# A Mamba-2 and attention trunk: four head pairs to one TensorE visit, y written over the convolved x, and a longer planned distance for TensorE's side work

## The chip, the cores and the metric

The kernel runs on one core of one Trainium2 chip. The metric is the device time of one execution in microseconds (us). Before the change it is 1143.38 us, the median of three runs (1142.94 to 1145.92). The profile is of one execution of its own.

## What is computed

The input x is 256 rows of 2048 numbers in fp32. The first layer is a Mamba-2 layer, the second is attention; both add their result to the stream, and a norm ends the trunk.

```python
def mamba2_layer(h, w_in, ...):                 # h = rmsnorm(x), 256 x 2048
    proj = h @ w_in                             # 2048 x 10304: z, xBC (x, B, C), dt
    xbc = silu(causal_depthwise_conv(xbc, conv_w, conv_b))      # 4 taps
    dt = softplus(dt + dt_bias);  a = dt * -exp(A_log)
    y = ssd_chunked_scan(x * dt, a, B, C)       # one chunk of 256: per head,
        # y = ((C B^T) * exp(a_cum[l] - a_cum[s]), causal) @ (x * dt)
    y = y + D_skip * x                          # 64 heads of 64 channels, 8 groups
    y = grouped_rmsnorm(y * silu(z), gnorm_g)   # over each group's 512 channels
    return y @ w_out                            # 4096 x 2048
...
k, v = rope(..), ..  = split(rmsnorm(x) @ w_kv)            # 2048 x 4096
q, z = rope(..), ..  = split(rmsnorm(x) @ w_in)            # 2048 x 4096
x = x + (causal_attention(q, k, v) * silu(z)) @ w_out      # 16 heads of 128
out = rmsnorm(x)
```

With 256 rows there is one attention block, so the block selection of the reference picks nothing but that block.

## The kernel before

**Products.** All the big products run in blocks of 512 output columns. A block has two halves of 128 rows and goes through its weights in units of 256 rows by 512 columns. `load` brings a unit to the tile `raw` (four buffers), `split` makes of it `hi` (ScalarE rounds it to fp32r) and `lo` (VectorE takes the difference), and `products` issues three products of 512 columns for each 128 rows and each half: x-high by hi, x-low by hi, x-high by lo. There are 384 such units and so 4608 products, which all write tiles named `ps`. The list `ORDER` gives the order of the first layer's blocks; the second layer has four K, four V, and then the blocks "z0 q0 q1 z1 q2 q3 z2 z3" of gates and queries.

**Side work.** Everything else (convolution, decay matrices, norms, rope, attention) is written as generators. After each three products `some(2)` advances up to two of them by a step. `Paced` wraps TensorE, ScalarE and VectorE, adds up a planned time for each instruction, and so keeps three planned clocks while the program is being written out. `Side.some` advances a generator only if what it did last is planned to end `MARGIN` (750 ns) before TensorE's planned clock, and nothing at all while an engine is planned over `LAG` (1000 ns) ahead of TensorE. The order on each engine is fixed by this when the program is built; on the chip only semaphores hold it. Helper instructions all carry line 126, the line in `Paced` that calls the engine.

**The scan, group by group.** For each group g of eight heads (four pairs), `conv_gen` makes the convolved x in a slot `xs` and its transposed, dt-weighted copy `xd`; `cb_gen` makes C B^T (tile `cb`). A `pair_gen` for each pair copies two rows of a_cum over all partitions (a copy on the GpSimd queue from the small DRAM tensor `AC` to a slot `em`, 256 KB), takes the exponent and multiplies by `cb`. At every second pair it does TensorE's part for two pairs, in a PSUM bank each: eight matmuls with a 64-column stationary operand, two heads writing the two halves of the 128 partitions. I call such a stretch between products a visit. Then VectorE makes y = x*D + that, in a slot `yt`, and y*0.5*z with the gate. `norm_gen` squares, sums and normalizes y into the operand `yn`. Slots: `xs` three, `em` two, `yt` two, PSUM banks for side work (`s`) four.

**Between the layers.** `x1_gen` transposes the new stream by 128 columns (index k, 0 to 15) and writes the operand `kvop`; `r1_gen` computes the norm's factors, transposes them (`s<-ident,r`), copies them to `rB`, and writes `csr` (rope's table times the factor), then `bop`, the second layer's operand.

Of the kernel before, what the change touches and what calls it, by code (L numbers as in the profile page):

```python
# [15 lines left out]
P = 128  # L16
# [12 lines left out]
MAIN_BANKS = 4  # L29
LAG = 1000.0  # L30
MARGIN = 750.0


ORDER = "B0 d0 C0 x0 z0 x1 z1 x2 z2 x3 z3 B1 o0 C1 o1 x4 o2 z4 x5 o3 z5 x6 o10 z6 x7 o11 z7 o12 o13 p0 p1 p2 p3".split()
# [95 lines left out]
class Side:  # L130
# [8 lines left out]
    def advance(self, entry):  # L139
        gen, ready, _ = entry  # L140
        if ready is not None and not ready():
            return 0
        before = [e.ns for e in self.engines]
        at = 0.0
        try:
            entry[1] = next(gen)
            if isinstance(entry[1], float):
                at, entry[1] = entry[1], None
        except StopIteration:
            self.gens.remove(entry)  # L150
        entry[2] = max([at] + [e.ns for e, b in zip(self.engines, before) if e.ns > b])
        return 1

    def some(self, most):


        PE = self.engines[0]
        for entry in list(self.gens):
            if most <= 0 or any(e.ns > PE.ns + LAG for e in self.engines):
                return  # L160
            if entry[2] <= PE.ns - MARGIN:
                most -= self.advance(entry)

    def step(self):
# [5 lines left out]
def trunk_kernel(ctx: ExitStack, tc: tile.TileContext, x, a_norm_g, a_w_in, a_conv_w, a_conv_b,  # L170
# [31 lines left out]
    def dram(t, offset, ap):  # L202
# [6 lines left out]
    psum = ctx.enter_context(tc.tile_pool(name="psum", bufs=1, space=bass.MemoryType.PSUM))  # L209
    scratch = ExitStack()  # L210
    work = scratch.enter_context(tc.tile_pool(name="ssd", bufs=2, reuse_waits="tile"))
    S = [Slots(work, {"T": ([P, 512], 2), "u": ([P, 4, L], 1), "xs": ([P, 4, L], 3), "xd": ([P, 2, 512], 1),
                      "cb": ([P, 384], 4), "em": ([P, 2, 384], 2), "z": ([P, 1024], 1), "yt": ([P, 4, L], 2)})]
    banks = Slots(psum, {"s": ([P, 512], 8 - MAIN_BANKS)}, clock.banks)
    spare = Parts(big, "U", "y5", [P, 1024], 2)
    B = {}
# [5 lines left out]
        return next(s for s in (banks, S[0], spare) if tag in s.shape)  # L222

    def can(*tags):
        return lambda: all(of(t).free(t) > 0 for t in tags)

    def take(tag):
        return of(tag).take(tag)
# [177 lines left out]
        return a.rearrange("p j (b l) -> p j b l", l=32)  # L406


    ga = const.tile([16, P], F32, name="ga")
    SP.dma_start(ga, dram(a_norm_g, 0, [[P, 16], [1, P]]))  # L410
    xl = [big.tile([P, D], F32, name=f"xl{t}", tag=f"y{4 + t}") for t in range(2)]
    xv = x[0].rearrange("(t p) d -> p t d", p=P)
# [85 lines left out]
    warm_up()  # L498
    nt = const.tile([P, 4, 2], F32, name="r0")
    r0 = nt[:, 2, :]  # L500

    def squares(h):

# [4 lines left out]
    def first_norm():  # L508
        DVE.tensor_reduce(nt[:, 0, :], ss, axis=mybir.AxisListType.X, op=OP.add)
        root(nt, D)  # L510

    gv = const.tile([P, 112], F32, name="gv")
    cbias = const.tile([P, 48], F32, name="cbias")
# [63 lines left out]
    def dt_gen(w):  # L577
        u, m, e, s, s2 = (w[0:64, i, :] for i in range(5))
        DVE.scalar_tensor_tensor(m, u, -1.0, u, op0=OP.mult, op1=OP.min)
        yield  # L580
        ACT.activation(e, m, AF.Exp)
        yield
        DVE.tensor_scalar(m, e, 2.0, None, op0=OP.add)
        DVE.reciprocal(s2, m)
        DVE.tensor_mul(s, e, s2)
        yield
        DVE.tensor_mul(s2, s, s)
        DVE.tensor_scalar(m, s2, 1.0 / 17, None, op0=OP.mult)
# [24 lines left out]
        for t in range(2):  # L613
            PE.transpose(p[:, t, :], b[:, t * P:(t + 1) * P], ident)
        yield
        dal = const.tile([P, 2, P], F32, name="dal", tag="c2")
        ACT.activation(dal, p, AF.Copy)
        give(p)
        st["dal"] = dal
# [69 lines left out]
                side.add(cb_gen(q), lambda: ("B", q) in st and ("C", q) in st)  # L689
        return evac  # L690

    def pair_gen(g, j):

        c = 4 * g + j
        E = take("em")
        AC = st["AC"]
        R = bass.AP(tensor=AC.tensor, offset=AC.offset + 2 * c * L, ap=[[0, P], [L, 2], [1, L]])
        POOL.dma_start(E[:, :, :L], R)
        yield copied(E)
        yield lambda: "dal" in st  # L700
        dal = st["dal"]
        for h in range(2):
            a = 64 + 2 * c + h
            ACT.activation(E[:, h, 256:384], E[:, h, P:L], AF.Relu, bias=dal[:, 1, a:a + 1], scale=-1.0)
            ACT.activation(E[:, h, 0:256], E[:, h, 0:256], AF.Relu, bias=dal[:, 0, a:a + 1], scale=-1.0)
        ACT.activation(E, E, AF.Exp, scale=-1.0)
        yield lambda: ("cb", g) in st
        DVE.tensor_mul(E, E, st["cb", g][:, None, :].to_broadcast([P, 2, 384]))
        st["em", g, j], when["em", g, j] = E, clock.last
        if j % 2:  # L710
            yield lambda: ("xd", g) in st and ("em", g, j - 1) in st
            yield max(when["xd", g], when["em", g, j - 1])
            yield lambda: of("s").free("s") > 1 and (("y", g) in st or can("yt")())
            for i in (j - 1, j):
                xd, E, q = st["xd", g], st.pop(("em", g, i)), take("s")[:, :L]
                for h in range(2):
                    PE.matmul(q[h * 64:(h + 1) * 64, :], lhsT=xd[:, 0, i * P + h * 64:i * P + (h + 1) * 64],
                              rhs=E[:, h, 0:256], start=True, stop=False)
                for h in range(2):
                    PE.matmul(q[h * 64:(h + 1) * 64, P:L], lhsT=xd[:, 1, i * P + h * 64:i * P + (h + 1) * 64],  # L720
                              rhs=E[:, h, 256:384], start=False, stop=True)
                give(E)
                st["q", g, i], when["q", g, i] = q, clock.last
            if ("y", g) not in st:
                st["y", g], st["n", g] = take("yt"), 0
            yield
        else:
            yield lambda: ("q", g, j) in st
            yield when["q", g, j]
        xd, xs, q = st["xd", g], st["xs", g], st.pop(("q", g, j))  # L730
        y = st["y", g][:, j, :]
        DVE.scalar_tensor_tensor(y, xs[:, j, :], Dv[:, c:c + 1], q, op0=OP.mult, op1=OP.add)
        give(q)
        st["x", g] = st.get(("x", g), 0) + 1
        if st["x", g] == 4:
            give(xs, xd, st["cb", g])
        yield lambda: ("z", g) in st
        z = st["z", g]
        y = y.rearrange("p (b l) -> p b l", l=32)
        DVE.scalar_tensor_tensor(y, y, 0.5, by_channel(z)[:, j], op0=OP.mult, op1=OP.mult)  # L740
        st["n", g] += 1
        if st["n", g] == 4 and g not in (1, 3):
            give(z)

    def norm_gen(g):
# [37 lines left out]
    def z_gen(U, there, g):  # L783
# [5 lines left out]
        else:  # L789
            yield can("z")  # L790
            z = take("z")
        ACT.activation(z, U, AF.Tanh, scale=0.5)
        yield
        DVE.scalar_tensor_tensor(z, z, 1.0, U, op0=OP.add, op1=OP.mult)
        give(U)
# [1 line left out]

    def z_evac(g):
        def evac(ps, t):
            U, there = turn(ps, t, r0)  # L800
            if t:
                side.add(z_gen(U, there, g))
        return evac

    def x_evac(g):
        base = conv_evac(4 * g, ("xs", g), g)

        def evac(ps, t):
            base(ps, t)
            if not t:  # L810
                return
            for j in range(4):
                side.add(pair_gen(g, j), lambda: "AC" in st and can("em")())
            side.add(norm_gen(g), lambda: st.get(("n", g)) == 4)
        return evac

# [66 lines left out]
    def r1_gen():  # L883
# [16 lines left out]
        ACT.activation(rB, R, AF.Copy)  # L900
        give(R)
        yield
        csr = const.tile([P, 2, L], F32, name="csr", tag="c2")
        DVE.tensor_mul(csr, B["cs"], rB[:, None, :].to_broadcast([P, 2, L]))
        B["csr"] = csr
        bop = [big.tile([P, 4, 2 * L], F32R, name=f"bop{i}", tag=f"y{i}") for i in range(4)]
# [81 lines left out]
    def att_gen(half, there, h0):  # L988
# [57 lines left out]
                      start=False, stop=True)  # L1046
        give(E)
        yield
        if ("z", h0) not in st:
# [5 lines left out]
            yield lambda: ("z", h0) in st  # L1055
        gate = st.pop(("z", h0))
        DVE.tensor_mul(gate.heads, in_32s(o), gate.heads)
        give(o)
        yield
# [12 lines left out]
    def gate_gen(U, there, n):  # L1072
# [7 lines left out]
            DVE.scalar_tensor_tensor(U[:, c], th, 1.0, U[:, c], op0=OP.add, op1=OP.mult)  # L1080
            give(th)
        for i, half in enumerate(two(U)):
            st["z", 4 * n + 2 * i] = half

    def zb_evac(n):
        def evac(ps, t):
# [9 lines left out]
        block(w_kv, 2 * D, 512 * n, range(16), lambda k: B["kvop"][:, k, :], "x", k_evac(n), "kv")  # L1096
    for n in range(4):
        block(w_kv, 2 * D, D + 512 * n, range(16), lambda k: B["kvop"][:, k, :], "x", v_evac(n), "kv")
    for kind, n in ("z0", "q0", "q1", "z1", "q2", "q3", "z2", "z3"):
        n = int(n)  # L1100
        if kind == "q":
            block(b_w_in, 2 * D, 512 * n, range(16), b_op, "x", q_evac(n), "b")
# [145 lines left out]
```

## Time and profile before

| what | value |
|---|---|
| median of three runs | 1143.38 us |
| the profiled execution: its own time, its span | 1143.61 us, 1141.9 us |
| TensorE busy, share of the span | 99% |
| VectorE, ScalarE, GpSimd busy | 73%, 56%, 11% |
| granted TensorE clock, mean | 0.997 of full speed |
| moved from and to HBM, over the span | 226 GB/s |
| chain that ended last: `ps` products, side work of TensorE (`s`) | 90% and 6% of the span |

The span runs from the first to the last instruction; the own time of an execution has some time around it (1.7 us here). Matmuls are recorded with their latency and overlap, so what one costs is read from start to start, not from its duration. A matmul of two fp32 operands is recorded as two rows, so eight matmuls of a visit show as x16.

### The profile page before, as it was taken

What the parts mean: (1) busy time and instruction counts of PE and PEld (TensorE: products, weight loads), DVE (VectorE), ACT (ScalarE), POOL (GpSimd) and SP (SyncE); (2) the same over time, 40 slices, a digit from 0 to 9 for tenths busy, and PEclk for the clock granted to TensorE, in tenths of its full rate; (3) what the DMA queues carried; (4) which work ended last, traced back from release to release, by engine and by line L of the source; (5) the groups of instructions that cost most, each with busy time, mean ns of one, the idle gap of its engine ahead of it and who ended that gap; (6) DMA issues with size and microseconds to landing.
All of it is one profiled execution on the core that took longest, in us unless ns stands there. A gap on an engine that the chain in (4) does not pass through costs nothing.

```text
span 1141.9 us, 14900 instructions
## 1 busy us (share of the span) xinstructions
PE 1130.1 (99%) x5217; PEld 923.2 (81%) x5217; DVE 839.2 (73%) x1283; ACT 641.6 (56%) x890; POOL 124.4 (11%) x217
## 2 busy tenths in 40 slices
PE   9999999999999999999999999999999999999996
PEld 6888888888888888888878888888888888888885
DVE  5787878778799878787877558876445597887564
ACT  5666566767656666667554655434343444445353
POOL 2011112012011111101000000000000012122000
PEclk9999999999999999999999999999999999999998
DMA  8787888878778777777765467768658688888852
GB/s 263 222 242 242 249 229 278 268 243 253 210 222 240 223 237 225 237 234 231 215 232 177 162 197 218 224 200 261 220 174 244 209 248 237 263 250 261 254 185 92
DMA packets 130363, 258.91 MB, mean 227 GB/s; under 512 B 12976, under 2 KB 13824, under 8 KB 129904
## 3 DMA queue, kind: packets, MB, share of 16 engines
q1 hardware_dynamic: 119232, 226.01, 63.2%
q0 software_dynamic: 11056, 31.95, 10.9%
q8 instruction: 41, 0.67, 0.2%
q14 instruction: 34, 0.28, 0.1%
HBM read 235.83 MB, written 22.09 MB: 226 GB/s over the span
## 4 chain that ended last, share of the span: by engine, by line
PE 96%; DMA 1%; DVE 1%; ACT 0%; SPq 0%; issue 0%; ACTq 0%; DVEq 0%
PE ps L126 90%; PE s L126 6%; DMA raw<-in_a_w_in_dram 1%; PE ps_dt L126 0%; DVE xs L126 0%; DVE lo L126 0%; ACT hi L126 0%; SPq L416 0%; DVE x L126 0%; DVE T L126 0%; SPq L306 0%; ACT T L126 0%; ACT x L126 0%; DVE sfin L126 0%; ACTq L1243 0%
## 5 line engine op out<-in xcount | busy, mean ns | idle before, releaser
L126 DVE TENSOR_TENSOR lo<-raw,hi 128x1024 fp32r<-128x1024 f32 (+1 forms) x385 | 462.7, 1215 | 192.1 <-ACT hi L126 189.1
L126 ACT ACTIVATE hi<-raw 128x1024 fp32r<-128x1024 f32 (+1 forms) x385 | 397.7, 1052 | 263.3 <-PE ps L126 137.5
L126 PE MATMUL ps<-hi,hT 128*128 128x512 f32 x1280 | 401.1, 394 | 0.5 <-ACT hi L126 0.4
L126 PEld LDWEIGHTS ps<-hi,hT 128*128 128x128 f32 x1280 | 235.6, 188 | 49.2 <-issue 2.1
L126 PE MATMUL ps<-lo,hT 128*128 128x512 f32 x640 | 249.8, 390 | 0.0
L126 PE MATMUL ps<-hi,bop 128*128 128x512 f32 x512 | 161.1, 396 | 0.0
L126 PE MATMUL ps<-hi,yn 128*128 128x512 f32 x512 | 159.7, 393 | 0.0
L126 PE MATMUL ps<-hi,kvop 128*128 128x512 f32 x512 | 158.2, 390 | 0.0
L397 POOL DMA_DIRECT2D U<-turned x128 | 74.3, 587 | 748.9 <-DMA turned<-T 408.2
L126 PEld LDWEIGHTS ps<-lo,hT 128*128 128x128 f32 x640 | 120.1, 188 | 26.4 <-DVE lo L126 0.9
L126 PEld LDWEIGHTS ps<-hi,kvop 128*128 128x128 f32 x512 | 95.7, 188 | 19.7
L126 PEld LDWEIGHTS ps<-hi,bop 128*128 128x128 f32 x512 | 95.8, 188 | 19.4
L126 PEld LDWEIGHTS ps<-hi,yn 128*128 128x128 f32 x512 | 94.7, 188 | 19.4 <-issue 0.5
L126 PE MATMUL ps<-lo,yn 128*128 128x512 f32 x256 | 99.8, 390 | 0.0
L126 PE MATMUL ps<-lo,bop 128*128 128x512 f32 x256 | 99.8, 390 | 0.0
L126 PE MATMUL ps<-lo,kvop 128*128 128x512 f32 x256 | 99.7, 389 | 0.0
L126 PE MATMUL ps<-hi,oop 128*128 128x512 f32 x256 | 78.9, 390 | 0.0
L126 DVE STREAM_TRANSPOSE T<-ps 128x512 f32<-128x512 f32 x64 | 43.4, 699 | 25.6 <-ACT ps L126 15.9
L126 DVE SCALAR_TENSOR_TENSOR xs<-u,cw,xs 128x255 f32<-128x255 f32 (+2 forms) x144 | 59.7, 475 | 0.0
L126 ACT ACTIVATE em<-em,dal 128x128 f32<-128x128 f32 (+1 forms) x128 | 54.4, 449 | 5.0 <-DMA em<-AC 2.9
L126 PEld LDWEIGHTS ps<-lo,bop 128*128 128x128 f32 x256 | 48.0, 188 | 10.3
L126 PEld LDWEIGHTS ps<-lo,yn 128*128 128x128 f32 x256 | 48.0, 188 | 10.1
(165 smaller groups left out, 922.5 us busy)
## 6 DMA issues: line engine op xcount, KB each, us to landing
raw<-in_a_w_in_dram SPq DMA_DIRECT2D x159, 512.0 KB, 5.3
raw<-in_a_w_out_dram SPq DMA_DIRECT2D x64, 512.0 KB, 4.8
raw<-in_w_kv_dram SPq DMA_DIRECT2D x64, 512.0 KB, 4.8
raw<-in_b_w_in_dram SPq DMA_DIRECT2D x64, 512.0 KB, 4.7
turned<-T SPq DMA_DIRECT2D x64, 256.0 KB, 4.3
U<-turned POOLq DMA_DIRECT2D x128, 128.0 KB, 6.5
raw<-in_b_w_out_dram SPq DMA_DIRECT2D x32, 512.0 KB, 4.9
em<-AC POOLq DMA_DIRECT2D x32, 256.0 KB, 6.0
```

The source lines that it names most:

```text
L126: return call(out, *args, **kw)
L397: POOL.dma_start(U[32 * q:32 * q + 32].rearrange("p (b c) -> p b c", b=8), src)
```

## The change

- `MARGIN_PE`, 3000 ns: a step that waits for a PSUM bank (`can` with "s"), that is TensorE's side work, is advanced only if what its generator did last is planned to end 3000 ns before TensorE's planned clock. Other steps keep 750 ns. `advance` no longer forgets an earlier planned end at a step that issues nothing.
- `pair_gen` is split. `em_gen` makes the decay matrix of one pair. `y_gen` waits for all four pairs of a group, takes two PSUM banks and issues all sixteen matmuls (32 recorded rows) in one visit, two pairs to a bank. VectorE writes y over the convolved x in `xs`, and multiplies by the gate for two pairs at a time.
- Slots: `xs` four, `em` four, `yt` none. Four `em` copies can be under way at once where two could.
- The 0.5 of the gate moves to the factor `r0h` that scales z, and out of the tanh and the last product.
- `ga` and `dal` share another constant slot, and `csr` gets a place of its own. Attention's gates have the name "gate" in the table `st`, where "z" was also the first layer's. The second layer's blocks stand as "z0 q0 q1 q2 z1 q3 z2 z3".

```diff
+MARGIN_PE = 3000.0
...
-        entry[2] = max([at] + [e.ns for e, b in zip(self.engines, before) if e.ns > b])
+        entry[2] = max([entry[2], at] + [e.ns for e, b in zip(self.engines, before) if e.ns > b])
...
-            if entry[2] <= PE.ns - MARGIN:
+            if entry[2] <= PE.ns - (MARGIN_PE if getattr(entry[1], "pe", False) else MARGIN):
                 most -= self.advance(entry)
...
-    S = [Slots(work, {"T": ([P, 512], 2), "u": ([P, 4, L], 1), "xs": ([P, 4, L], 3), "xd": ([P, 2, 512], 1),
-                      "cb": ([P, 384], 4), "em": ([P, 2, 384], 2), "z": ([P, 1024], 1), "yt": ([P, 4, L], 2)})]
+    S = [Slots(work, {"T": ([P, 512], 2), "u": ([P, 4, L], 1), "xs": ([P, 4, L], 4), "xd": ([P, 2, 512], 1),
+                      "cb": ([P, 384], 4), "em": ([P, 2, 384], 4), "z": ([P, 1024], 1)})]
...
     def can(*tags):
-        return lambda: all(of(t).free(t) > 0 for t in tags)
+        def ready():
+            return all(of(t).free(t) >= tags.count(t) for t in tags)
+        ready.pe = "s" in tags
+        return ready
...
+        DVE.tensor_scalar(r0h, r0, 0.5, None, op0=OP.mult)
...
         st["em", g, j], when["em", g, j] = E, clock.last
...
-            yield lambda: of("s").free("s") > 1 and (("y", g) in st or can("yt")())
-            for i in (j - 1, j):
-                xd, E, q = st["xd", g], st.pop(("em", g, i)), take("s")[:, :L]
...
+    def y_gen(g):
+
+        yield lambda: ("xd", g) in st and st.get(("ems", g)) == 4
+        yield max(when["xd", g], *(when["em", g, j] for j in range(4)))
+        yield can("s", "s")
+        xd, y = st["xd", g], st["xs", g]
+        Q = []
+        for i in (0, 2):
+            q = take("s").rearrange("p (j l) -> p j l", j=2)
+            Q.append(q)
+            for j in (i, i + 1):
+                E = st.pop(("em", g, j))
                 for h in range(2):
+                    PE.matmul(q[h * 64:(h + 1) * 64, j - i, :], lhsT=xd[:, 0, j * P + h * 64:j * P + (h + 1) * 64],
                               rhs=E[:, h, 0:256], start=True, stop=False)
...
-        DVE.scalar_tensor_tensor(y, xs[:, j, :], Dv[:, c:c + 1], q, op0=OP.mult, op1=OP.add)
...
-        DVE.scalar_tensor_tensor(y, y, 0.5, by_channel(z)[:, j], op0=OP.mult, op1=OP.mult)
...
+                DVE.scalar_tensor_tensor(y[:, j, :], y[:, j, :], Dv[:, c:c + 1], Q[i // 2][:, j - i, :],
+                                         op0=OP.mult, op1=OP.add)
+            give(Q[i // 2])
...
+            DVE.tensor_mul(v, v, by_channel(z)[:, i:i + 2])
...
-        csr = const.tile([P, 2, L], F32, name="csr", tag="c2")
+        csr = p.tile([P, 2, L], F32, name="csr", bufs=1)
...
-    for kind, n in ("z0", "q0", "q1", "z1", "q2", "q3", "z2", "z3"):
+    for kind, n in ("z0", "q0", "q1", "q2", "z1", "q3", "z2", "z3"):
```

The change adds one line above the helpers, so line 126 of before is line 127 of the change.

The first place is TensorE's first visit for y (`s<-em,xd`, of group 0) among the products (`ps`). Before:

```order
L126 MATMUL ps<-lo,hT 128x512
L126 MATMUL s<-em,xd 64x256 x2
L126 MATMUL s<-em,xd 64x128 x2
L126 MATMUL s<-em,xd 64x256 x2
L126 MATMUL s<-em,xd 64x128 x2
L126 MATMUL ps<-hi,hT 128x512 x2
```

In the change, at the same place:

```order
L127 MATMUL ps<-lo,hT 128x512
L127 MATMUL s<-em,xd 64x256 x2
L127 MATMUL s<-em,xd 64x128 x2
L127 MATMUL s<-em,xd 64x256 x2
L127 MATMUL s<-em,xd 64x128 x2
L127 MATMUL s<-em,xd 64x256 x2
L127 MATMUL s<-em,xd 64x128 x2
L127 MATMUL s<-em,xd 64x256 x2
L127 MATMUL s<-em,xd 64x128 x2
L127 MATMUL ps<-hi,hT 128x512 x2
```

The first layer has 16 visits of the first kind before, and 8 of the second kind in the change; the matmuls in them are the same in number and shape.

The second place is TensorE in the first K block, where the norm's factors are transposed (`s<-ident,r`). Before, the last transposes of the stream (`s<-ident,x`, k = 15) stand six groups of three products ahead of it:

```order
L126 MATMUL ps<-hi,kvop 128x512 x2
L126 MATMUL ps<-lo,kvop 128x512
L126 MATMUL s<-ident,r_6034 128x128 x2
L126 MATMUL ps<-hi,kvop 128x512 x2
L126 MATMUL ps<-lo,kvop 128x512
```

In the change:

```order
L127 MATMUL s<-ident,r_6020 128x128 x2
L127 MATMUL ps<-hi,kvop 128x512 x2
L127 MATMUL ps<-lo,kvop 128x512
L127 MATMUL ps<-hi,kvop 128x512 x2
L127 MATMUL ps<-lo,kvop 128x512
L127 MATMUL s<-ident,x_1480 128x128
L127 MATMUL s<-ident,x_1481 128x128
L127 MATMUL ps<-hi,kvop 128x512 x2
L127 MATMUL ps<-lo,kvop 128x512
```

The transposes for k = 15 now come two groups behind the factors, and the first products that read k = 15 are the fourth group after them; before, fifteen groups lay between.

The third place is VectorE there, from the table `csr` on. Before:

```order
L126 TENSOR_SCALAR r1h<-r_6034 128x2
L126 TENSOR_TENSOR lo<-raw,hi 128x1024
L126 TENSOR_TENSOR csr<-cs,rB 128x512
L126 SCALAR_TENSOR_TENSOR x1T_5512<-x1T_5512,gv,rB 128x256 x2
L126 TENSOR_TENSOR lo<-raw,hi 128x1024
```

In the change:

```order
L127 SCALAR_TENSOR_TENSOR kvop<-s,gv,kvop 128x256
L127 TENSOR_TENSOR lo<-raw,hi 128x1024
L127 TENSOR_TENSOR csr<-cs,rB 128x512
L127 SCALAR_TENSOR_TENSOR x1T_5474<-x1T_5474,gv,rB 128x256 x2
L127 SCALAR_TENSOR_TENSOR kvop<-s,gv,kvop 128x256
L127 TENSOR_TENSOR bop_6107<-x1T_5474,bop_6107 128x2x256
```

The low half of k = 15 (the second `kvop` row) now stands behind `csr` and two rows that wait for `rB`; before, it stood ahead of them.

## Rows read from the trace of the kernel before

**Rows 1.** Page, part 5: costliest groups: ScalarE's hi (busy, mean ns | idle before).

```profile
L126 ACT ACTIVATE hi<-raw 128x1024 fp32r<-128x1024 f32 (+1 forms) x385 | 397.7, 1052 | 263.3 <-PE ps L126 137.5
```

**Rows 2.** TensorE's waits, whole span: us in total, times, longest.

```profile
PE s L126 <- DVE early L126: 1.2, 1, 1.2
PE s L126 <- DMA xl<-in_x_dram: 0.5, 1, 0.5
PE ps L126 <- ACT hi L126: 0.4, 1, 0.4
```

**Rows 3.** Chain of waits: start us, us, what.

```profile
689.20 228.51 PE ps L126 x1008
1132.52 0.02 issue
```

**Rows 4.** Timeline, TensorE, first visit for y: start us, us.

```profile
139.76 0.39 PE L126 MATMUL ps<-lo,hT 128*128 128x512 f32 x1
140.08 1.52 PE L126 MATMUL s<-em,xd 128*64 128x256 f32 x16
141.53 0.73 PE L126 MATMUL ps<-hi,hT 128*128 128x512 f32 x2
142.10 0.39 PE L126 MATMUL ps<-lo,hT 128*128 128x512 f32 x1
```

**Rows 5.** Timeline, TensorE, inside that visit (narrow windows, last heads and second pair).

```profile
140.67 0.49 PE L126 MATMUL s<-em,xd 128*64 128x128 f32 x4
...
140.78 0.39 PE L126 MATMUL s<-em,xd 128*64 128x256 f32 x2
...
141.32 0.28 PE L126 MATMUL s<-em,xd 128*64 128x128 f32 x2
```

**Rows 6.** Timeline, TensorE, a visit for y with cb matmuls behind it.

```profile
355.73 0.39 PE L126 MATMUL ps<-lo,hT 128*128 128x512 f32 x1
356.05 1.52 PE L126 MATMUL s<-em,xd 128*64 128x256 f32 x16
...
358.72 0.40 PE L126 MATMUL ps<-lo,hT 128*128 128x512 f32 x1
```

**Rows 7.** Timeline, TensorE, the first and the second visit for cb.

```profile
98.98 0.39 PE L126 MATMUL ps<-lo,hT 128*128 128x512 f32 x1
...
100.71 0.40 PE L126 MATMUL ps<-lo,hT 128*128 128x512 f32 x1
...
110.25 0.39 PE L126 MATMUL ps<-lo,hT 128*128 128x512 f32 x1
...
111.58 0.39 PE L126 MATMUL ps<-lo,hT 128*128 128x512 f32 x1
```

**Rows 8.** Timeline, TensorE, two visits of a norm's squares.

```profile
235.36 0.39 PE L126 MATMUL ps<-lo,hT 128*128 128x512 f32 x1
...
236.27 0.39 PE L126 MATMUL ps<-lo,hT 128*128 128x512 f32 x1
...
303.32 0.40 PE L126 MATMUL ps<-lo,hT 128*128 128x512 f32 x1
...
304.36 0.40 PE L126 MATMUL ps<-lo,hT 128*128 128x512 f32 x1
```

**Rows 9.** Timeline, TensorE, ScalarE and VectorE, from the factors' transposes on.

```profile
688.82 0.38 PE L126 MATMUL s<-ident,r 128*128 128x128 f32 x2
...
689.29 0.39 ACT L126 ACTIVATE rB<-s 128x256 f32<-128x256 f32 x1 [0.42 <-PE s L126]
...
690.31 0.68 DVE L126 TENSOR_TENSOR csr<-cs,rB 128x512 f32<-128x512 f32 x1
690.91 0.87 DVE L126 SCALAR_TENSOR_TENSOR x1T<-x1T,gv,rB 128x256 f32<-128x256 f32 x2
...
686.09 0.48 DVE L126 SCALAR_TENSOR_TENSOR kvop<-s,gv,kvop 128x256 fp32r<-128x256 f32 x1
```

**Rows 10.** Windows: us, busy of PE, PEld, DVE, ACT, POOL, clock, DMA share, GB/s.

```profile
100.00:300.00 200.00, 200.00 (x955) 162.88 (x954) 154.68 (x233) 134.09 (x182) 28.23 (x46) 1.00 0.85 251
```

More of the change, by code (lines that the diff above doesn't have):

```diff
@@ L406, in in_32s @@
         return a.rearrange("p j (b l) -> p j b l", l=32)
-    ga = const.tile([16, P], F32, name="ga")
+    ga = const.tile([16, P], F32, name="ga", tag="c1")
     SP.dma_start(ga, dram(a_norm_g, 0, [[P, 16], [1, P]]))
@@ L500, in trunk_kernel @@
     r0 = nt[:, 2, :]
+    r0h = const.tile([P, 2], F32, name="r0h")
     def squares(h):
@@ L615, in dt_gen @@
         yield
-        dal = const.tile([P, 2, P], F32, name="dal", tag="c2")
+        dal = const.tile([P, 2, P], F32, name="dal", tag="c1")
         ACT.activation(dal, p, AF.Copy)
@@ L690, in c_evac, with em_gen @@
         return evac
-    def pair_gen(g, j):
+    def em_gen(g, j):
         c = 4 * g + j
@@ L709, in pair_gen @@
         st["em", g, j], when["em", g, j] = E, clock.last
-        if j % 2:
-            yield lambda: ("xd", g) in st and ("em", g, j - 1) in st
-            yield max(when["xd", g], when["em", g, j - 1])
-            yield lambda: of("s").free("s") > 1 and (("y", g) in st or can("yt")())
-            for i in (j - 1, j):
-                xd, E, q = st["xd", g], st.pop(("em", g, i)), take("s")[:, :L]
+        st["ems", g] = st.get(("ems", g), 0) + 1
+        if st["ems", g] == 4:
+            give(st["cb", g])
@@ L718, in pair_gen @@
                               rhs=E[:, h, 0:256], start=True, stop=False)
                 for h in range(2):
-                    PE.matmul(q[h * 64:(h + 1) * 64, P:L], lhsT=xd[:, 1, i * P + h * 64:i * P + (h + 1) * 64],
+                    PE.matmul(q[h * 64:(h + 1) * 64, j - i, P:L], lhsT=xd[:, 1, j * P + h * 64:j * P + (h + 1) * 64],
                               rhs=E[:, h, 256:384], start=False, stop=True)
                 give(E)
-                st["q", g, i], when["q", g, i] = q, clock.last
@@ L724, in pair_gen @@
-            if ("y", g) not in st:
-                st["y", g], st["n", g] = take("yt"), 0
+        give(xd)
+        for i in (0, 2):
             yield
[L727 to L731, printed above, removed]
-        DVE.scalar_tensor_tensor(y, xs[:, j, :], Dv[:, c:c + 1], q, op0=OP.mult, op1=OP.add)
-        give(q)
-        st["x", g] = st.get(("x", g), 0) + 1
@@ L735, in pair_gen @@
-        if st["x", g] == 4:
-            give(xs, xd, st["cb", g])
+            for j in (i, i + 1):
+                c = 4 * g + j
+                DVE.scalar_tensor_tensor(y[:, j, :], y[:, j, :], Dv[:, c:c + 1], Q[i // 2][:, j - i, :],
+                                         op0=OP.mult, op1=OP.add)
+            give(Q[i // 2])
         yield lambda: ("z", g) in st
         z = st["z", g]
-        y = y.rearrange("p (b l) -> p b l", l=32)
-        DVE.scalar_tensor_tensor(y, y, 0.5, by_channel(z)[:, j], op0=OP.mult, op1=OP.mult)
@@ L741, in pair_gen @@
-        st["n", g] += 1
-        if st["n", g] == 4 and g not in (1, 3):
+        for i in (0, 2):
+            v = y[:, i:i + 2, :].rearrange("p j (b l) -> p j b l", l=32)
+            DVE.tensor_mul(v, v, by_channel(z)[:, i:i + 2])
+            yield
+        st["y", g] = y
+        st["n", g] = 4
+        if g not in (1, 3):
             give(z)
@@ L791, in z_gen @@
             z = take("z")
-        ACT.activation(z, U, AF.Tanh, scale=0.5)
+        ACT.activation(z, U, AF.Tanh)
         yield
@@ L799, in evac @@
         def evac(ps, t):
-            U, there = turn(ps, t, r0)
+            U, there = turn(ps, t, r0h)
             if t:
@@ L812, in evac @@
             for j in range(4):
-                side.add(pair_gen(g, j), lambda: "AC" in st and can("em")())
+                side.add(em_gen(g, j), lambda: "AC" in st and can("em")())
+            side.add(y_gen(g))
             side.add(norm_gen(g), lambda: st.get(("n", g)) == 4)
@@ L1048, in att_gen @@
         yield
-        if ("z", h0) not in st:
+        if ("gate", h0) not in st:
             yield can("q")
@@ L1054, in att_gen @@
             o = z
-            yield lambda: ("z", h0) in st
-        gate = st.pop(("z", h0))
+            yield lambda: ("gate", h0) in st
+        gate = st.pop(("gate", h0))
         DVE.tensor_mul(gate.heads, in_32s(o), gate.heads)
@@ L1082, in gate_gen @@
         for i, half in enumerate(two(U)):
-            st["z", 4 * n + 2 * i] = half
+            st["gate", 4 * n + 2 * i] = half
     def zb_evac(n):
```

1 line of the change is left out of this document (removed).

## The prediction

> **What bounds the kernel now.** I read the waits of TensorE first. Over the whole span it waits by name three times, 2.1 us in all, and of its products only one, for 0.4 us, waits for the weights' high half [rows 2]; all three lie in the start, before the stream of products is under way. ScalarE, which makes that half, idles 263 us, and over half of this until TensorE frees a buffer [rows 1]: the weights run ahead of TensorE, not behind it. The chain of waits says the same: one piece of 1008 products without anything between takes 228.51 us, 0.2267 us for one, and the chain is on TensorE until 1132.52 us, from where on only the last rows are finished and stored [rows 3]. So 4608 products take 1044.6 us whatever is done elsewhere, and time can only be won or lost in what stands between the products: the side work's own columns, what a change from one kind of matmul to another costs, and pauses in which TensorE's next side work isn't ready. VectorE, ScalarE and the queues count only where they make such a pause. I therefore read the timeline of TensorE visit by visit, from the start of the last product in front of a visit to that of the third behind it; three products alone take 3 x 0.2267 = 0.68 us, and the rest is the visit's price.
>
> **Four pairs to a visit.** The first visit for y, two pairs, takes 142.10 - 139.76 = 2.34 us, so its price is 1.66 us [rows 4]. Inside it a pair in full flow costs 0.65: 0.54 from the second pair's start to the start of its last two heads, and 0.11 from such a start to the next pair, as between the pairs [rows 5]. Two pairs are 1.30, so 0.36 us of the price is paid once for the visit: 0.09 before its first matmul, 0.10 between its last heads and the product behind (0.21 instead of 0.11), and the rest in the first pair and the first products behind. The other 15 visits for y look alike. The change has 8 visits of four pairs with the same matmuls: 4 x 0.65 + 0.36 = 2.96 each, against 2 x 1.66 = 3.32. It saves 8 x 0.36 = 2.9 us. No trace of before has a visit of four pairs. The low end is nothing saved, if the 0.36 is paid for each two pairs or each bank; that the pairs inside one visit follow at 0.11, though they lie in two banks, speaks against it [rows 5]. The high end is the same 2.9, as the 0.65 is array work. I take 2.9, since the row it comes from is the operation itself.
>
> What is the 0.36 paid for? One visit has cb's matmuls right behind it. It takes 358.72 - 355.73 = 2.99, less 0.68 is 2.31 [rows 6]: 1.66 and the 0.66 of a cb visit that stands alone (111.58 - 110.25 - 0.68, [rows 7]). So joining unlike matmuls saves nothing; only like ones share the price. The Trainium skill, TensorEngine Tiling (Array Packing), section Key Properties, says that changing the tiling mode drains the engine, though not another tile of the same mode. The 0.09 in front and the 0.10 behind are such a drain; by that rule alone the sum would be 8 x 0.19 = 1.5 us instead of 2.9, and the time 1141.3. No run here has yet one such change of mode less, so between the two I go by the row's 0.36.
>
> **Side work farther from what it needs.** The first cb visit takes 1.73 us where the next takes 1.33 [rows 7]: TensorE waits 0.4 us for VectorE's convolved C. In the order of the change this visit stands two groups of three products, 1.36 us, later, and what it waits for is unmoved, so the pause goes. A squares visit at 303 us takes 1.04 where another takes 0.91 [rows 8]: 0.13 us, which goes too, as every visit of TensorE is now planned 3 us behind its input and the largest pause seen is 0.4. Pauses under 0.1 us I don't count. Together 0.5 us; the bounds are 0 and 0.7.
>
> What is late next? The steps come later, so the slots are held longer, and each later consumer is nearer. One place is tight: the first K block. There the transposes of k = 15 have only three groups to the first product that reads them, and VectorE's low half stands behind `csr`. Counted from the start of the factors' transposes, TensorE reaches the product that needs this half after two visits of transposes (0.23 each, [rows 8]), five groups (3.40) and one product (0.23): 4.1 us. The other path is 0.47 to the start of `rB`, 0.39 for it, 0.60 to the next rows, 0.87 and 0.48 [rows 9]: 2.8 us. That leaves 1.3 us, so I take 0; a weight split of VectorE that comes late in front of `csr` would show as a pause of what it exceeds 1.3 by.
>
> **The rest, at nothing.** VectorE loses 32 products with 0.5 and the gate and gains 16 of twice the width and `r0h`; ScalarE loses a scale operand in the tanh; both are covered by TensorE, on which no product waits for `lo` at all, and while all of 100 to 300 us is TensorE's, VectorE is busy 155 of 200 us [rows 10]. With that cover gone, `r0h` would cost its own two-column step, some tenths of a us, once. The moved query block changes which attention heads find their gate ready; TensorE's matmuls are the same. Slots and names cost no instruction. Four `em` copies can be in flight where two were: on the GpSimd queue the copies of U now stand behind up to four of them. What waits for U is a convolution or a gate, whose products come many us later.
>
> **Sum.** 1143.61 - 2.9 - 0.5 = 1140.2 us for the profiled execution, and the median of the runs lies 0.23 below it: 1140.0. With the pauses under 0.1 us, which can only go, I say 1139.9.
>
> **Rivals.**
> - *The price is paid for each two pairs, in whole or part.* For it: a new bank begins there. Against it: pairs follow in 0.11 over a change of bank [rows 5]. Nothing saved leaves 1143.4 - 0.5 = 1142.9; half, 1141.4. Chance 0.14.
> - *A new pause takes back part.* The k = 15 place, or another consumer that came nearer. For it: only 1.3 us are spare there. Against it: VectorE idles about a quarter of the time [rows 10] and the weights it splits are early [rows 1]. A pause of 0.5 to 2 us: 1140.4 to 1141.9. Chance 0.08.
> - *More comes off than I see*, 0.5 to 1 us, if the first products behind a visit or the start gain as well: 1139.2. Chance 0.07. Against it: all pauses named in the trace are in the sum.
> - *Slower: the burst of `em` copies starves the weights.* Four copies of 256 KB are 1.05 MB. At 251 GB/s in all [rows 10], if half goes to the copies, the burst lasts 8.4 us, in which the weights get 125 GB/s and need 193 (512 KB for every 12 products, 2.72 us); they fall back 2.9 us, against 1.5 for two copies. Where the lead of the weights is under that, each of eight groups costs up to 1.5 us more: 1140 + 12 = 1152. It decides from the point at which products wait for `hi` or `lo` in every group. Against it: with bursts of two, no product waited after the start [rows 2]. The Trainium skill, DMA: Bandwidth & Descriptors, section Queues, rings and completion order, says that each DMA engine takes turns between queues by packets, which would make the half a fair share; no run here shows it yet. Chance 0.04.
>
> **How the numbers follow.** The forecast has 0.67; its own range is 1139.0 to 1140.8. I hold 0.3% (3.4 us, so 1139.95) for what a measurement of this kernel can tell from no change, and the forecast lies on that line: of its 0.67 I put 0.43 below and 0.24 above. With the 0.07 of "more" that is 0.50 for faster; 0.24, 0.14 and 0.08 make 0.46 for within 0.3%; slower has 0.04. The range for 8 in 10 goes from 1138.8, a little below "more", to 1142.9, nothing saved by the visits.
>
> **What would show it.** In the changed profile: eight visits of x32 for `s<-em,xd`, each 2.96 us by the same reading (3.3 if the price is per two pairs); the first cb visit at 0.66; the piece of products per 0.2267 us unchanged; no wait of TensorE by name after the start; the product of k = 15 in the first K block without a pause. The stream's end should stand at about 1129.1 us instead of 1132.5. I am wrong if the visits cost 3.3, if TensorE pauses at `kvop`, or if products wait for `hi` or `lo` after a burst of `em`.

## The result, and the profile after

The changed kernel takes 1152.08 us (median of four runs, 1149.66 to 1153.91); beside it the kernel before took 1143.89. The ratio is 1.0068, 95% interval 1.0044 to 1.0091: slower by 8 us, where 4 us faster was forecast. The profiled execution took 1151.84 us, with a span of 1150.1.

TensorE's waits, to be held against [rows 2]: us in total, times, longest. Of the tiles, `nt` holds a norm's factors, `Es` attention's exponentials, which come back from the DRAM tensor `turned_E`, and `lo` is the low half of the weights.

```profile
PE s L127 <- DVE nt L127: 2.6, 1, 2.6
PE ps L127 <- DVE lo L127: 2.4, 3, 1.8
PE s L127 <- DMA Es<-turned_E: 1.5, 2, 0.9
PE s L127 <- DVE early L127: 1.2, 1, 1.2
PE s L127 <- DVE xs L127: 0.6, 1, 0.6
```

Where before waited by name only in its start, seven waits of four kinds now stand in the stream. The page's row on the chain that ended last gives each engine's share of the path (TensorE had 96% before):

```profile
PE 71%; DMA 12%; DVE 10%; issue 3%; ACT 3%; POOL 1%; DVEq 0%; SPq 0%; ACTq 0%; POOLq 0%
```

Three pieces of that chain, to read like [rows 3] (start us, us, what):

```profile
169.40 13.57 DMA raw<-in_a_w_in_dram
...
780.04 8.96 DMA U<-turned
795.92 127.68 PE ps L127 x562
```

12% of the path are now copies. ScalarE, in the page's row on its rounding of the weights, idles longer than before and is no busier [rows 1]: its input comes later.

```profile
L127 ACT ACTIVATE hi<-raw 128x1024 fp32r<-128x1024 f32 (+1 forms) x385 | 396.5, 1052 | 283.1 <-PE ps L127 102.8
```

The visits themselves came out. Timeline of TensorE around the first one for y (start us, us), to read like [rows 4]:

```profile
145.41 0.39 PE L127 MATMUL ps<-lo,hT 128*128 128x512 f32 x1
145.73 2.82 PE L127 MATMUL s<-em,xd 128*64 128x256 f32 x32
148.48 0.73 PE L127 MATMUL ps<-hi,hT 128*128 128x512 f32 x2
149.06 0.39 PE L127 MATMUL ps<-lo,hT 128*128 128x512 f32 x1
```

149.06 - 145.41 - 0.68 = 2.97 us; 2.96 was forecast. The other visits for y show 2.96 too (one, with a norm's transposes joined on, 3.18). So 2.9 us were saved and some 11 lost.

To find the 11, I took each product's distance to the next matmul's start (and that of a side matmul to the product behind it) over what this pair of neighbours usually takes, and added it up by stage. The unit is us. Small sums are in every kernel, and they hang by some 2 us on what is taken as usual, for all kernels alike.

| kernel | 20-100 | 100-300 | 300-620 | 620-700 | 700-900 | 900 on | all |
|---|---|---|---|---|---|---|---|
| before | 1.2 | 1.0 | 2.2 | 1.2 | 0.0 | 3.2 | 8.8 |
| changed | 0.8 | 7.4 | 1.8 | 1.4 | 2.7 | 5.4 | 19.4 |
| e5 | 0.8 | 1.2 | 1.7 | 1.4 | 2.5 | 4.8 | 12.4 |
| e9 | 1.3 | 1.3 | 1.9 | 1.2 | 1.8 | 3.5 | 11.0 |
| e11 | 0.9 | 1.0 | 2.1 | 1.2 | 0.0 | 3.1 | 8.2 |
| e13 | 0.9 | 1.2 | 1.7 | 1.4 | 0.7 | 5.2 | 11.0 |

19.4 - 8.8 - 2.9 = 7.7 against a span that is 8.2 longer. The largest piece is at 183 to 197 us:

```profile
185.46 0.50 PE L127 MATMUL ps<-lo,hT 128*128 128x512 f32 x1 [0.31 <-DVE lo L127]
...
191.31 0.39 PE L127 MATMUL ps<-lo,hT 128*128 128x512 f32 x1
194.27 0.66 PE L127 MATMUL s<-ident,nt 128*128 128x128 f32 x2 [2.56 <-DVE nt L127]
194.58 1.20 PE L127 MATMUL ps<-hi,hT 128*128 128x512 f32 x2
195.58 0.63 PE L127 MATMUL ps<-lo,hT 128*128 128x512 f32 x1
```

It begins with the weights. Among the DMA issues of 168 to 170 us are two 1 MB copies of x and one load of weights (count, KB each, median us to landing):

```profile
x<-in_x_dram POOLq DMA_DIRECT2D x2, 1024.0 KB, 12.7
raw<-in_a_w_in_dram SPq DMA_DIRECT2D x1, 512.0 KB, 13.6
```

The load took 13.6 us where 5.4 is the median of this matrix; VectorE's splits bunch up behind it, and the norm's small steps stand among them.

### The profile page after: what moved, and what is told of

Same layout as the page of the kernel before. It is cut to its first block, busy times and chain, and to the rows that moved or that the text cites. A ratio compares the mean times of both kernels' runs of the same rounds, so it can differ in the third digit from the quotient of the medians.

```text
span 1150.1 us, 14868 instructions
## 1 busy us (share of the span) xinstructions
PE 1132.3 (98%) x5217; PEld 925.8 (81%) x5217; DVE 836.7 (73%) x1268; ACT 639.8 (56%) x889; POOL 126.2 (11%) x217
## 4 chain that ended last, share of the span: by engine, by line
PE 71%; DMA 12%; DVE 10%; issue 3%; ACT 3%; POOL 1%; DVEq 0%; SPq 0%; ACTq 0%; POOLq 0%
PE ps L127 66%; PE s L127 4%; DVE lo L127 3%; DMA raw<-in_a_w_in_dram 3%; DMA U<-turned 3%; DMA turned<-T 3%; DVE T L127 2%; ACT hi L127 1%; DMA turned_E<-PT 1%; DVE Es L127 1%; DVE K L127 1%; DMA Es<-turned_E 1%; DVE xs L127 1%; ACT em L127 1%; DMA raw<-in_b_w_in_dram 1%
## 5 line engine op out<-in xcount | busy, mean ns | idle before, releaser
L127 DVE TENSOR_TENSOR lo<-raw,hi 128x1024 fp32r<-128x1024 f32 (+1 forms) x385 | 463.0, 1215 | 198.0 <-ACT hi L127 195.4
L127 ACT ACTIVATE hi<-raw 128x1024 fp32r<-128x1024 f32 (+1 forms) x385 | 396.5, 1052 | 283.1 <-PE ps L127 102.8
L127 PEld LDWEIGHTS ps<-lo,kvop 128*128 128x128 f32 x256 | 48.1, 188 | 13.2 <-DVE lo L127 3.2
```

Source lines behind the costliest of these rows:

```text
L127: return call(out, *args, **kw)
```

## The experiments

All times are medians, and each ratio is to runs of the kernel before on the same chip (medians 1143.6 to 1144.1). A difference between runs of unlike batches, such as e5 and the changed kernel, is one between chips. "Lost" is the sum of the table above.

**Which part of the change?** e1 brings the residual x in pieces:

```diff
-            POOL.dma_start(B["x1"][t], xv[:, t])
+            for h in range(4):
+                POOL.dma_start(B["x1"][t][:, h * 512:(h + 1) * 512], ...)   # 256 KB, each paced
```

> The change, with one edit: the stream x for the second residual, two copies of 1 MB back to back on the GpSimd queue, is loaded as eight copies of 256 KB, each planned at least 8 us behind the one before. Theory A (bursts of copies meet weights that run too close ahead): in the changed kernel a weight load issued right behind the two copies took 13.6 us and TensorE lost 3.6 us at a norm's transposes, 0.6 us at lo and 1.0 us at the lower clock between 184 and 197 us, 5.2 us together; that goes, 1152.1 - 5.2 = about 1147 (1146 to 1148.5). Theory B (the longer margin shifts the side work so that VectorE and ScalarE come late, whatever the copies do): under 1 us, 1151 to 1153.

1148.86 us, ratio 1.0035 (1.0022 to 1.0048). The pause at 194 us is gone (100 to 300 us lost 1.8), but 8.8 were lost from 900 us on. The loss showed at the x copies, but most of it stayed without them.

e2 undoes the block order:

```diff
-    for kind, n in ("z0", "q0", "q1", "q2", "z1", "q3", "z2", "z3"):
+    for kind, n in ("z0", "q0", "q1", "z1", "q2", "q3", "z2", "z3"):
```

> The change, with one edit: the second layer's blocks stand as z0 q0 q1 z1 q2 q3 z2 z3 again. In the changed kernel two visits of attention's last matmuls (Es,V, at 994 and 1048 us) pause 1.1 and 0.9 us for the copy of Es, and 0.2 us are lost to the clock behind. If the block order makes the queue of copies there: about 2 us come back, 1150 (1149.3 to 1150.8). If the pauses come from the margins or from how the copies fall in a run: no difference that can be told, 1151 to 1153.

1149.95 us, ratio 1.0050 (1.0030 to 1.0070); 8.1 lost from 900 us on. Not the order.

e3 undoes the planned distance:

```diff
-MARGIN_PE = 3000.0
+MARGIN_PE = 750.0
-        entry[2] = max([entry[2], at] + ...
+        entry[2] = max([at] + ...
```

> The change, with the order model as before: 750 ns for TensorE's side work too, and the planned end forgotten at steps that issue nothing; visits of four pairs, slots, y over x and the block order stay. Theory B: the margins are the cause, so nearly all of the 8 us goes and the visits' 2.9 us are left as a gain: 1140.5 to 1143. Theory A: the four em copies and the x copies still come in bursts, so most of the loss stays: 1148 to 1152.

1150.23 us, ratio 1.0056 (1.0041 to 1.0071). The losses moved (6.3 at 300 to 620 us, in many small waits) and did not go.

e4 lets only two `em` copies be under way:

```diff
-  side.add(em_gen(g, j), lambda: "AC" in st and can("em")())
+  side.add(em_gen(g, j), lambda j=j: "AC" in st and can("em")() and (j < 2 or ("cp", g, j - 2) in st))
```

> The change, with one edit: the em copies of pairs 2 and 3 of a group are issued only when those of pairs 0 and 1 are planned to have landed, so two are in flight as before. Theory A, with the em burst as its beginning: the weights' lead, 2 to 4 us from 95 to 170 us where it was 4 to 6, comes back, and the x copies find it larger; 1146 to 1149. If only the x copies matter: 1151 to 1153. Theory B: 1151 to 1153.

1160.26 us, ratio 1.0138 (1.0120 to 1.0157). Taking the burst away makes it worse, as the decay matrices come later: 5.7 us were lost at 622 to 630 us, where products wait for `yn`. So this run adds a loss of its own; the better evidence against my burst rival is e5 below, which keeps the burst and is 8 us faster.

**The addresses.** Every part undone left 4.7 us or more, and in each there were waits for `lo` at 700 to 900 us, where the kernel before has none and where, from `csr` to the first query block, e3 has the order of before on every engine and queue. Two things all four shared: the four-pair visits with their slots, and the place of their tiles in SBUF. Of the constants at its start the change gives up 512 bytes (`ga`) and 2048 (`csr`), ten times 256, and adds 32 for the two columns of `r0h`. Everything behind moves by 2528 bytes: `raw` begins 192 bytes beyond a multiple of 256 before (a multiple of 64), and 224 beyond one in the change (32 beyond a multiple of 64).

e5 is the changed kernel with one line more, and no other difference:

```diff
+    pad = const.tile([P, 8], F32, name="pad")      # 32 bytes, never used
```

> The changed kernel with 32 bytes of unused constant ahead of all other tiles; the order on every engine is the same. In the kernel before, the tiles raw, hi, lo, U, em and xs begin at multiples of 64 bytes in SBUF; the change's edits of the small constants moved all of them to 32 beyond one, and this puts them back. Theory 'address': copies that land 32 bytes off a multiple of 64 take longer, which makes raw, U and em late; then this kernel's weight pauses shrink wherever they stand, the two or so us of waits for lo at 700 to 900 us go, and it takes 1141 to 1145. Theory 'copies': the pauses come from copies bunched against a small lead of the weights, which is the same here; then 1149 to 1153, with 7 us lost at 100 to 300 as before.

1143.95 us, ratio 1.0004 (0.9993 to 1.0014): 8.1 us off for 32 unused bytes, or 7.3 by the ratios. The pad does not put the tiles back to 192 beyond a multiple of 256 but on to a multiple of it; no run has the changed kernel at 192. Its waits of TensorE:

```profile
PE ps L127 <- DVE lo L127: 1.8, 3, 0.8
PE s L127 <- DVE early L127: 1.2, 1, 1.2
PE s L127 <- DMA Es<-turned_E: 1.0, 2, 0.9
PE ps L127 <- ACT hi L127: 0.2, 1, 0.2
```

The wait for `nt` is gone, with x still loaded by two copies of 1 MB. These and the loads of weights beside them land sooner (DMA issues of 164 to 168 us in e5):

```profile
x<-in_x_dram POOLq DMA_DIRECT2D x2, 1024.0 KB, 10.2
raw<-in_a_w_in_dram SPq DMA_DIRECT2D x2, 512.0 KB, 6.6
```

The theory was wrong in one point: the waits for `lo` at 700 to 900 us stayed, so the clue that led me to the addresses was not their doing. The engines themselves are not slowed by the place: `hi` and `lo` take 1052 and 1215 ns a piece in the changed kernel, 1052 and 1216 in e5.

e6 puts the same line into the kernel before.

> The kernel before with the same 32 bytes of unused constant, which moves its tiles to 32 beyond a multiple of 64 as in the change; nothing else differs. Theory 'address': 1147 to 1152, with waits for lo at 700 to 900 us, where it has none now. Theory 'copies': 1143 to 1145, as it is.

1147.95 us, ratio 1.0032 (1.0022 to 1.0042): 4 us slower with nothing else touched. Its profiled execution was the fastest of ten (1144.38), so that trace shows little of the 4 us: one wait for `lo`, of 0.3 us, where the theory wanted several. But copies have 5% of its chain that ended last, against 1% before:

```profile
PE 88%; DMA 5%; DVE 3%; issue 2%; ACT 1%; POOL 0%; SPq 0%; ACTq 0%; DVEq 0%; POOLq 0%
```

e7 gives the kernel before the longer planned distance alone (the first hunks of the change, and the mark on its visits).

> The kernel before with only the longer planned distance: the 3000 ns for TensorE's side steps and the planned end that is no longer forgotten; two pairs to a visit, slots and block order stay as before. Theory 'address': TensorE's waits stay few, 1142 to 1145. Theory 'copies' in the form that the later side work takes the weights' lead: pauses of several us, 1147 to 1151.

1162.04 us, ratio 1.0163 (1.0149 to 1.0176): both expectations missed. One wait of TensorE makes most of it (timeline, with the idle time before it):

```profile
591.27 1.64 PE L127 MATMUL s<-em,xd 128*64 128x256 f32 x16
603.86 0.66 PE L127 MATMUL s<-ident,nt 128*128 128x128 f32 x2 [10.95 <-DVE nt L127]
```

I read it so that with two slots for `em` the later visits hold them longer, and the last group's chain is not done in time; no run tests this. In the changed kernel, with its four slots, the distance costs nothing (e5 against e9).

e8 is e5 with x in pieces.

> The changed kernel with the 32 bytes of e5 and, as in e1, the residual x brought in eight paced pieces of 256 KB instead of two of 1 MB. Theory 'address' with the x copies as a second cause: 1139 to 1142, below the kernel before by up to 5. Theory 'copies': as e1, 1147 to 1151.

1143.76 us, ratio 1.0002 (0.9987 to 1.0017). As e5; once the tiles lie well, the x copies are no second cause. Against e1 the 32 bytes are worth 5.1 us.

**Which multiple, and the rest.** e9 is e3 with the 32 bytes, e12 is e2 and e3 together with them, so that of the change the visits, slots and constants are left.

> The changed kernel with the 32 bytes of e5 and the old planned distance (750 ns for every step, an earlier planned end forgotten): four pairs to a visit, slots, y over x and the new block order stay. e7 showed the longer distance to cost the kernel before 18 us by itself. Theory 'address and margin' (misplaced tiles cost 8 us, the longer distance takes back what the visits save): the 2.9 us of the visits now come out, 1139 to 1142. Theory 'bunching' (four copies at once and four pairs in a row are what costs the rest): as e5, 1143 to 1146.

> As e9, and with the old order of the second layer's blocks: of the change only the four-pair visits, the slots, y over x and the moved constants are left, with the tiles at multiples of 64. Theory 'address and margin': 1139 to 1142, as e9; if the block order matters at all, the two differ at 900 to 1150 us. Theory 'bunching': 1143 to 1146.

e9: 1143.68 us, ratio 0.9994 (0.9977 to 1.0011), 6.5 below e3. e12: 1142.96, ratio 0.9984 (0.9968 to 1.0001). The distance and the block order thus change next to nothing here, and the 2.9 us of the visits still don't come out: both medians lie above the 1139 to 1142 of my theory. e9 is in the range of "bunching"; but TensorE's waits in e12 are short single ones at unlike places (`lo` 1.0, `Es` 0.9, `nt` 0.8, `squares`, the input of a norm's factors, 0.6), not one kind in every group. Its profiled execution, of 1145.53 us, was slower than its median.

e10 has 96 bytes in place of 32 (`raw` 64 beyond a multiple of 256), e11 is the kernel before with 64 (`raw` at a multiple of 256).

> The changed kernel with 96 bytes in place of the 32 of e5: the tiles raw, hi, em and xs begin at 64 beyond a multiple of 256 bytes instead of at one. Theory '64': a multiple of 64 is enough, as e5, 1142 to 1146. Theory '256': copies to a place off a multiple of 256 are dearer, so part of the 8 us stays, 1147 to 1152.

> The kernel before with 64 bytes of unused constant: raw, hi, em and xs move from 192 beyond a multiple of 256 bytes to a multiple of 256. Theory '64': no change, 1143 to 1145. Theory '256': the kernel before was itself held up by this and gets faster, 1140 to 1142.5.

e10: 1147.34 us, ratio 1.0027 (1.0007 to 1.0047), between the changed kernel and e5. e11: 1142.96, ratio 0.9982 (0.9969 to 0.9995): the kernel before was itself held up a little, and this is the one version whose interval lies below both. So the loss goes by degrees, and a multiple of 64 is not enough; a place 128 beyond a multiple of 256 was not run. With its tiles at a multiple of 256 the kernel before (1142.96) is no slower than the changed one (1143.95): at equal places the change gains nothing.

The pages show it in the DMA queues (packets, MB, share of 16 engines' span) and in the landing of `em` (count, KB, median us). Before:

```profile
q1 hardware_dynamic: 119232, 226.01, 63.2%
q0 software_dynamic: 11056, 31.95, 10.9%
...
em<-AC POOLq DMA_DIRECT2D x32, 256.0 KB, 6.0
```

The changed kernel:

```profile
q1 hardware_dynamic: 119232, 226.01, 63.4%
q0 software_dynamic: 11056, 31.95, 11.2%
...
em<-AC POOLq DMA_DIRECT2D x32, 256.0 KB, 8.0
```

e5:

```profile
q1 hardware_dynamic: 119232, 226.01, 62.4%
q0 software_dynamic: 11056, 31.95, 10.5%
...
em<-AC POOLq DMA_DIRECT2D x32, 256.0 KB, 6.3
```

The same packets and bytes take 72.9% of the engines' time in e5 and 74.6% in the changed kernel, whose span is longer too. The records of single packets agree: those of 4096 bytes on q0 have a median of 173 ns in e5 and 174 in e11, 201 in before, 211 in e10, 220 in the changed kernel and in e6. What the place costs inside a copy they do not show: e7, whose tiles lie as before's, has 220 too, the fastest tenth takes 159 ns in all seven, and the weights' packets of 2048 bytes, by far the most, have a median of 84 ns in all of them (the mean is 103 in e5 and 105 in the changed kernel). So much of the difference can be packets waiting for each other.

**Why e5 isn't at 1140.** A block of K or V goes through the DRAM tensor `turned` to be rearranged. In e5, e9 and e12 the second K block's copies to `turned` land late, and a fetch of 16 KB of instructions stands among them (at 721.2, 721.8 and 723.4 us). The DMA view of 716.5 to 724 us in e5 (issues: count, KB, median us to landing):

```profile
q1 hardware_dynamic: 826, 1.56, 66.5%
q8 instruction: 1, 0.02, 0.8%
...
turned<-T SPq DMA_DIRECT2D x2, 256.0 KB, 6.1
```

e13 moves the fetches by cutting two warm-up products of TensorE into eight pieces each; e14 does the same to e11, which prices the cut.

```diff
-    warm_up()
+    for i in range(8):
+        PE.matmul(warm[:, i * 64:(i + 1) * 64], lhsT=w, rhs=w[:, :64], start=True, stop=True)
```

> e5 (the changed kernel, tiles at multiples of 256 bytes) with the first two warm-up products of TensorE cut into eight pieces each: 14 matmuls more ahead of the stream, which moves the places where TensorE's code is fetched some 6 us earlier in the work behind them. In e5, e9 and e12 a fetch of 16 KB falls at 721 to 723 us into the second K block's copies of 'turned', which take 5.9 to 6.4 us there and 3.9 to 4.3 in the kernel before, where the fetch ends ahead of them. Theory 'fetch': these copies take some 4 us, the waits for lo at 725 to 790 us (2.5 us in e5) shrink to under 1, and it takes 1141 to 1142.5. Theory 'not the fetch': the waits stay, 1143 to 1145.

> e11 (the kernel before, tiles at multiples of 256 bytes) with the same cut of the warm-up products. It prices the cut itself: 1142.5 to 1143.5, as e11, in both theories.

The cut costs more than I expected: e14 takes 1145.89 us, 2.9 more than e11 (3.4 when each is held against the kernel before on its own chip); its first product starts 3.5 us later. e13 takes 1145.47, ratio 1.0018 (1.0007 to 1.0029); less the 2.9 it would be 1142.5. The same copies in e13 (719.5 to 726 us):

```profile
q1 hardware_dynamic: 830, 1.57, 74.7%
...
turned<-T SPq DMA_DIRECT2D x2, 256.0 KB, 4.6
```

No fetch, 1.5 us less, and the loss at 700 to 900 us falls from 2.5 to 0.7. The other traces agree on the copies: in the ten of the four-pair kernel with a fetch among them they take 4.7 to 6.5 us, in e13 and e15, without one, 4.5 to 4.6. And e12, which has the order of before on every engine in this stretch, takes 5.9 with a fetch at 723.4 where e11, with the fetch ahead of them at 718.5, takes 4.0 to 4.3. But slow copies alone don't make the waits: in e10 they take 5.7 us, and 700 to 900 us lose only some 0.6.

e15 also plans `s<-Es,V` 2000 ns later; e16 was to bring a fetch into those copies of e11 with 29 pieces.

> e13 with attention's products for the heads (s<-Es,V) planned 2000 ns later behind their copies, since in e5 TensorE waits there for the copy of Es (0.9 us at 1040 us, 1.0 in all) and in the kernel before the same copy lands 0.4 us ahead of its use. If the fetch theory and this hold together, both rests of e5 go and the forecast's 1139.9 is reached: 1139.5 to 1141. If the later place makes something else late: as e13 or slower, 1142 to 1145.

> e11 with the two warm-up products in 29 pieces each: 56 matmuls more, which should bring a code fetch into the second K block's copies of 'turned', as in e5. The start gets longer by 1 to 4 us for the pieces alone. Theory 'fetch': these copies take some 6 us instead of 4, and waits for lo appear at 725 to 795 us, where e11 has none. Theory 'not the fetch': copies of 4 us and no waits there.

e15: 1146.62 us. The wait for `Es` went, and one for `oop`, the operand of the last products, came in its place (waits of TensorE: us, times, longest), with 3.9 us lost around it:

```profile
PE ps L127 <- ACT oop L127: 1.4, 1, 1.4
```

e16: 1165.15 us, with its first product 21 us later; its fetches fell at 715.3 and 745.9, beside the copies (740.2 to 745.3, which took 4.5), so it tells nothing of the fetch. It has one wait for `lo`, of 1.2 us, all the same, at the fourth K block. That the fetch delays the copies is therefore shown by taking it away, not by bringing it in.

## Why the prediction was wrong

**The step that failed** is "The rest, at nothing", and in it "Slots and names cost no instruction". That is true, and it was priced by its instructions. The 32 bytes of `r0h`, which I priced as a two-column step of some tenths of a us, moved the tiles that the copies write, `raw`, `U` and `em` among them, from 192 to 224 beyond a multiple of 256 bytes. That move alone costs 4.0 us in the kernel before (e6); in the changed kernel only the whole way from 224 to a multiple of 256 was run, and it gives 8.1 (e5), and 5.1 and 6.5 in two variants (e1 to e8, e3 to e9). No trace of before shows it; the places of the tiles in the two kernels do.

**A second step failed with it:** "What is late next?", taken at 0. With the tiles well placed e5 still lies 4 us above the forecast, as TensorE waits 1.8 us for `lo` and 1.0 for `Es`. That is the rival "a new pause takes back part", at other places than the one I named, and twice the 2 us that I allowed it at most.

The Trainium skill, DMA: Bandwidth & Descriptors, section How a descriptor splits into AXI transactions, says that a transaction starts at a multiple of 256 bytes, so that a descriptor beginning elsewhere carries bytes it doesn't use. It states this of reads. For copies into SBUF the times agree: 1143.95 us at a multiple of 256, 1152.08 at 224 beyond one. That bytes are carried in vain there no run shows; the median of the larger packets, 173 against 220 ns, can also be waiting.

**Visits for y:** right, 2.97 against 2.96 us. The rival by which each two pairs pay is out.

**Old pauses:** not as sized. The first cb visit takes 101.81 - 100.19 - 0.68 = 0.94 us in the timeline of the changed kernel, not 0.66: of the 0.4 to be won 0.28 is still lost. In e1, e2 and e5, with the same place in the order, it takes 0.65, as forecast, so the order did its part.

```profile
100.19 0.39 PE L127 MATMUL ps<-lo,hT 128*128 128x512 f32 x1
...
101.81 0.40 PE L127 MATMUL ps<-lo,hT 128*128 128x512 f32 x1
```

**The k = 15 place:** right. The first products that read it start at 698.23, in step with the group ahead:

```profile
695.95 0.38 PE L127 MATMUL s<-ident,x 128*128 128x128 f32 x2
...
698.00 0.39 PE L127 MATMUL ps<-lo,kvop 128*128 128x512 f32 x1
698.23 0.61 PE L127 MATMUL ps<-hi,kvop 128*128 128x512 f32 x2
698.68 0.39 PE L127 MATMUL ps<-lo,kvop 128*128 128x512 f32 x1
```

**"No product waits for lo":** the covers held with the copies and the order of that trace; they do not hold with slower copies, nor in e5, where three products wait for `lo`, 1.8 us in all. In 100 to 300 us TensorE was busy for all of the 200 us [rows 10]; now it isn't:

```profile
100.00:300.00 200.00, 196.48 (x932) 159.25 (x931) 154.26 (x226) 133.92 (x187) 28.37 (x46) 0.99 0.86 252
```

**The slower rival** named 1152, and 1152 it is, by another mechanism: products did not wait in every group but at three places, and e5, with the same bursts, has none of the 8 us. A right number there was chance.

**The rest to 1140.** e5 saves 2.9 and loses 12.4 - 8.8 = 3.6 more than before, so it stands where before stands. 2.5 of it are from 700 to 900 us, the K blocks' waits for `lo`, most of which go when the code fetches are moved (e13), and 1.6 are from 900 us on, where the copy of `Es` lands 0.4 us ahead of its use in e11 and is late by 0.9 in e5. e15 only moved that loss. Why the four-pair kernels e5, e12 and e13 wait for it (0.9 to 1.8 us at the longest) and e9 doesn't stays open.

## What to carry to other kernels

Before an edit is priced at nothing because it issues nothing, compare where the tiles lie: a constant of 32 bytes ahead of the big buffers can cost more than the edit saves, and here a pad of a few bytes put that part right. Where each undone part leaves the loss in place, look for what all variants share. And a saving of 3 us is worth its number only where a copy's lead, here 0.4 us for `Es` in e11, doesn't take it back.

## What was not expected of the hardware

- The place of a copy's destination: by residue of `raw`, `hi`, `em` and `xs` to 256 bytes, two-pair kernels took 1142.96 (0), 1144.0 (192) and 1147.95 (224), four-pair kernels 1143.95 (0), 1147.34 (64) and 1152.08 (224). Which of these tiles it is was not separated, nor how a copy loses the time.
- TensorE's code comes by 41 fetches of 16 KB (queue q8), 0.9 to 2.3 us each, which the page counts on the same 16 DMA engines as the data. The Trainium skill, Runtime: NRT & Kernel Launch, section Instruction fetch mechanics, calls the cost mostly hidden; in e5 one fetch stood among copies that took 6.1 us instead of 4.6.
- After the pause at 191.5 to 194.2 us the granted clock was 0.50, the lower level of 1.2 GHz, until 197.2 (windows, columns as in [rows 10]: the clock is the last but two): two products took 1.00 us from start to start where 0.46 is usual, so the pause of 2.6 us cost about 1.3 more.

```profile
191.50:194.20 2.70, 0.20 (x1) 0.00 (x0) 2.46 (x11) 0.00 (x0) 2.39 (x5) 0.95 0.87 250
194.30:197.20 2.90, 2.90 (x8) 2.41 (x9) 2.68 (x4) 1.78 (x2) 0.58 (x1) 0.50 0.92 223
197.30:200.00 2.70, 2.70 (x13) 2.25 (x12) 2.70 (x5) 1.30 (x2) 0.00 (x0) 0.99 0.97 230
```
